# Last eight output blocks with the last pair included, and key products of a recurrence on GpSimd

## The chip, the cores and the metric

The kernel runs on one core of one Trainium2 chip. The metric is device time in microseconds of that core, for one launch that takes all weights and tables from HBM.

## The reference, cut to what matters

The model has two blocks on 256 tokens of width 2048, in float32. The first block (a mixture of gating, short convolution and dilated attention, then a wide MLP) is not touched. The second block is

```python
h = rmsnorm(x, norm1_w); p = h @ w_in
z_rwkv, q, k, v = jnp.split(p, IN_SPLITS, axis=-1)
y_rwkv = rwkv7_bidir(z_rwkv, ...)                  # 16 heads of 64, forward and backward
y_attn = axial_gqa(q, k, v, q_norm_w, k_norm_w)    # 16 query heads, rotary embedding
x = x + jnp.concatenate([y_rwkv, y_attn], axis=-1) @ w_out
h2 = rmsnorm(x, norm2_w)
x = x + peer_ffn(h2, w_pq, sub_keys, u_tab, v_tab)
out = rmsnorm(x, normf_w)
```

Inside the recurrence the keys of a direction are `k_dir = k * (1 + (a - 1) * k_a)` and `ka = kk * a`, with `a` a sigmoid for each direction; the bonus takes the mean of `k_dir` over both directions. The rotary embedding is `x * cos + rotated(x) * sin`.

## The kernel before, in words

The residual x lies transposed: 16 tiles of 128 features by 256 tokens. A projection to 128 features is a "block": `stage` loads 128 x 1024 weights at a time with a DMA from SP (four buffers), ACT rounds them to a high part wH and DVE subtracts it to get the low part wL (L334, L335; three buffers of each), and `product` multiplies: the inputs are stored as pairs of a high and a low part, so that each 128-row step takes one matmul of 512 columns with wH (L344) and one of 256 columns with wL (L346), all into one accumulator of PSUM (two of them, tag acc).

Program order is not the order on the engines: a scheduler lays out each engine's queue ahead of time from priorities (program order at first) and its own costs, and each engine then runs its queue strictly in that order, with semaphores where data are needed.

The second block, in program order: projections of keys and values of the attention (two key blocks with rotary embedding, `rope`), low-rank inputs, then eight pairs of heads p = 0 to 7. For a pair there are three generators that are advanced by the string PLAN: C is the recurrence itself (`rwkv_chain`), B prepares the next pair's matrices (`rwkv_prep`), A makes the projections for the pair after that and its attention heads (`feed`, `gqa`). In `rwkv_prep`, for each direction, the decay is summed by a matmul (L875) and exponentiated on ACT (L882, L884), the keys are formed (L888 on ACT, then products, tile ak), two sets of small matmuls take them (L902 to ms, L909 transposes), and M, ATK and so on are stored for the chain. `tt` is an elementwise operation of two tensors (L251 in the profile); its engine is DVE unless one is named.

For pairs 6 and 7, where nothing is left to project, the places of A are taken by the output projection (`out_blocks`): its first 16 blocks (wo2a) take the eight attention tiles, the next 16 (wo2b) take the first seven pairs; two blocks run at each place, and what is left runs after the chain of pair 7. Then the last pair's result is split into its high and low parts, and 16 one-wide products (wo2c) add it. After each of them `n4.add` scales the finished tile of x (ACT L400, DVE L401) and sums its square over features: ACT squares it (L407) and two matmuls with ones add it up (L411); two buffers of squares alternate by the parity of the tile. Next come the query blocks of the expert layer (wpq, 16 steps each), which take all 16 scaled tiles, and the blocks of the expert table (ut).

Of the kernel before, what the change touches and what calls it, by code (L numbers as in the profile page):

```python
# [28 lines left out]
ADD, SUB, MUL = ALU.add, ALU.subtract, ALU.mult  # L29

P = 128
# [5 lines left out]
NS = 10  # L37
PLAN = "BCCBAABCABCAC"
OUTS = 2
GATED = 2  # L40
PRI = 300
AHEAD = 4
# [30 lines left out]
    ORD1 += [("c", _i, 14 + _i), ("x", _i, 20 + _i), ("b", _i, 8 + _i)]  # L73
KORD1 = list(range(10, 16)) + list(range(0, 10))

ORD2 = [("gk", 0, 37), ("gk", 1, 38), ("gv", 0, 39), ("gv", 1, 40)]
ORD2 += [("lo", _i, 24 + _i) for _i in range(3)] + [("gl", _i, 27 + _i) for _i in range(2)]
for _i in range(8):
# [87 lines left out]
def pack_inputs(inp):  # L166
    A = {k: np.asarray(v) for k, v in inp.items()}
    asc = np.ascontiguousarray
    r = {}

    def cols(v):
        return v.reshape(-1, P).T

    def dup(v):
        return np.concatenate([v.reshape(64, 1), v.reshape(64, 1)], 0)

    def blocks(w, order=None):
        kk, n = w.shape
        b = w.reshape(kk // P, P, n // P, P).transpose(2, 1, 0, 3)
        return b if order is None else b[order]  # L180

    r["xT"] = asc(A["x"][0].T.reshape(16, P, T).transpose(1, 0, 2))
    parts = {
        "attn_norm": cols(A["attn_norm"][0]), "mlp_norm": cols(A["mlp_norm"][0]),
        "norm1": cols(A["norm1_w_2"][0]), "norm2": cols(A["norm2_w_2"][0]),
        "conv_w": cols(A["conv_w"][0]),
        "qn1": dup(A["q_norm"][0]), "kn1": dup(A["k_norm"][0]),
        "qn2": dup(A["q_norm_w_2"][0]), "kn2": dup(A["k_norm_w_2"][0]),
        "mu_prev": cols(A["mu_prev_2"][0]), "mu_next": cols(A["mu_next_2"][0]),
        "a0": cols(A["a0_2"][0]), "k_k": cols(A["k_k_2"][0]), "k_a": cols(A["k_a_2"][0]),  # L190
        "r_k": cols(A["r_k_2"][0]), "lnx_w": cols(A["lnx_w_2"][0]), "lnx_b": cols(A["lnx_b_2"][0]),
    }
    r["vec"] = asc(np.concatenate([parts[n] for n, _ in _VEC], 1))
    r["w1"] = asc(blocks(A["w_in"][0], [o[2] for o in ORD1]))
    wo = A["w_out"][0].reshape(16, P, 2048)[KORD1].reshape(2048, 2048)
    r["wo1"] = asc(blocks(wo))
    r["wm1"] = asc(blocks(A["w_mlp_in"][0]))
    r["wm2"] = asc(A["w_mlp_out"][0].reshape(4, 16, P, 16, P).transpose(0, 3, 2, 1, 4))
    r["w2"] = asc(blocks(A["w_in_2"][0], [o[2] for o in ORD2]))
    wo2 = blocks(A["w_out_2"][0])  # L200
    r["wo2a"], r["wo2b"] = asc(wo2[:, :, 8:]), asc(wo2[:, :, :7])
    r["wo2c"] = asc(wo2[:, :, 7].transpose(1, 0, 2))
    r["wpq"] = asc(blocks(A["w_pq_2"][0]))
    r["ut"] = asc(A["u_tab_2"][0].reshape(P, P, 16, P).transpose(0, 3, 2, 1))
    for n in range(2):
        r[f"vt{n}"] = asc(A["v_tab_2"][0][:, n * 1024:n * 1024 + 1024])
    r["gf"] = asc(np.broadcast_to(A["normf_w_2"], (P, 2048)))
    r["sgw"] = asc(A["sgu_w"][0].transpose(2, 0, 1))
    r["sgb"] = asc(A["sgu_b"][0])
    r["skT"] = asc(A["sub_keys_2"][0].reshape(16, P, P).transpose(2, 0, 1))  # L210


    lora = np.zeros((8, P, 10, P), np.float32)
    w2, a2, g2 = A["w2_2"][0], A["a2_2"][0], A["g2_2"][0]

    def put(slot, r0, src):
        lora[:, r0:r0 + src.shape[0], slot, :] = src.reshape(src.shape[0], 8, P).transpose(1, 0, 2)

    put(0, 0, w2[0])
    put(1, 96, w2[1][:32])  # L220
    put(2, 0, w2[1][32:])
    put(3, 64, a2[0][:64])
    put(4, 0, a2[0][64:])
    put(5, 32, a2[1])
    put(6, 0, np.broadcast_to(A["w0_2"][0][0], (P, 1024)))
    put(7, 0, np.broadcast_to(A["w0_2"][0][1], (P, 1024)))
    put(8, 0, g2[:P])
    put(9, 0, g2[P:])
    r["lora"] = lora
    c = _consts()  # L230
    for n, names in (("cg", C_G), ("c1", C_1), ("cr", C_R), ("ch", C_H), ("cp", C_P)):
        r[n] = _pack(names, c)
    return r
# [6 lines left out]
def mega(tc, a, out):  # L240
# [150 lines left out]
    class Norm:  # L391


        def __init__(self, pool, gname, by_pe=False):
            self.pool, self.g, self.xs, self.acc, self.by_pe = pool, gname, [], None, by_pe

        def scale(self, j):
            x, g = cur["x"], vcol(self.g, j)
# [5 lines left out]
        def square(self, j, sq=None):  # L404
            if sq is None:
                sq = self.pool.tile([P, T], F32, name=nm("sq"), tag="ssq" if (j % 2 if self.by_pe else j == 0) else "nsq", bufs=1)
            S.activation(sq, cur["x"][j], AF.Square)  # L407
            if self.by_pe:
                if self.acc is None:
                    self.acc = ps((P, T))  # L410
                TE.matmul(self.acc, ones, sq, start=j == 0, stop=j == 15)  # L411
            elif self.acc is None:
                self.acc = sq
            else:
                tt(self.acc, self.acc, sq, ADD)
# [284 lines left out]
    def rope(d, o, q):  # L700
        s = ps((P, T))
        TE.matmul(s, cr["rot"], d, start=True, stop=True)
        tt(q, s, cr["sin"], MUL)
        tt(o, d, cr["cos"], MUL)
        tt(o, o, q, ADD)

    def gqa(i):
# [121 lines left out]
    def rwkv_prep(p, r, k, vpad, sws, aas):  # L829
# [41 lines left out]
        for d in range(2):  # L871
            sw, aa = sws[d], aas[d]
            cum = prep((P, 2, P))
            for t_ in range(2):
                TE.matmul(cum[:, t_], sw[:, t_], cr["trif" if d == 0 else "trib"], start=True, stop=True)  # L875
            cv = cum.rearrange("p a (b t) -> p (a b) t", b=2)
            pp = pr.tile([P, 4, 65], F32, name=nm("pp"), tag="pp")
            edge = 0 if d == 0 else 64
            V.memset(pp[:, :, edge:edge + 1], 1.0)
            cur = pp[:, :, 1:65] if d == 0 else pp[:, :, 0:64]  # L880
            prv = pp[:, :, 0:64] if d == 0 else pp[:, :, 1:65]
            S.activation(cur, cv, AF.Exp, scale=-DECAY)  # L882
            pi = c4(scr[("ra", "rb")[d]])
            S.activation(pi, cv, AF.Exp, scale=DECAY)  # L884
            V.tensor_copy(pc[:, d], pp[:, :, 64 - edge])

            kd = (bon, kd2)[d]
            S.activation(kd, aa, AF.Identity, bias=omka[:, p:p + 1], scale=vcol("k_a", p))  # L888
            tt(kd, kd, k, MUL)
            tt(aa, aa, kk, MUL)  # L890
            ak = pr.tile([P, 4, 3, 64], F32, name=nm("ak"), tag="ak")
            tt(ak[:, :, 0], c4(aa), pi, MUL)
            tt(ak[:, :, 1], c4(kd), pi, MUL)
            S.copy(ak[:, :, 2], ak[:, :, 0])
            if d == 1:
                tt(bon, bon, kd, ADD)
            tt(kr_[:, d, :, 0], c4(kk), prv, MUL)
            tt(kr_[:, d, :, 1], c4(r), cur, MUL)
            ms = [prep((P, 4, 2, 64)) for _ in rows]
            for c in range(4):  # L900
                for h, b in enumerate(rows):
                    TE.matmul(ms[h][:, c], ak[b, c, h:h + 2, :], kr_[b, d, c], start=True, stop=True)  # L902
            for h, b in enumerate(rows):
                tt(M[:, d, h], ms[h], ptm[:, d].unsqueeze(1).to_broadcast([P, 4, 2, 64]), MUL)

            tr = [prep((P, 4, P)) for _ in rows]
            for c in range(4):
                for h, b in enumerate(rows):
                    TE.transpose(tr[h][:, c], ak[:, c, h:h + 2, :].rearrange("p k t -> p (k t)"), ident)  # L909
            for h, b in enumerate(rows):  # L910
                S.copy(ATK[:, d, h], tr[h][:, :, b])
            if d == 0:
                yield
# [174 lines left out]

    def out_blocks(x):

        for name, ks in (("wo2a", range(8, 16)), ("wo2b", range(7))):
            for j in range(16):
                if j == 0:
                    reload(ks)
                if name == "wo2a":
                    nc.sync.dma_start(x[j], xd[j])
                acc = block(a[name][j], [y2[k] for k in ks])
                add_to(x[j], acc)
                yield
# [50 lines left out]
        for c in "CBA":  # L1150
            run(gens[c])
    run(outs)
    parts = stage(a["wo2c"], 16)
    last = split(yb[1])
    for j in range(16):
        H, L = (z[:, j % 8:j % 8 + 1] for z in parts[j // 8])
        acc = product([(H, L)], [last])
        add_to(x[j], acc)
        n4.add(j)
    rstd = n4.rstd()  # L1160
    closep(pr, psI, psP)
    psS = openp("psS2", bufs=6, space=PSUM)
# [91 lines left out]
    A = {}  # L1254
# [349 lines left out]
    with tc.If(over > R1):  # L1604
# [3 lines left out]
        for h in range(2):  # L1608
# [1 line left out]
    closep()  # L1610


_NAMES = ["xT", "vec", "w1", "wo1", "wm1", "wm2", "w2", "wo2a", "wo2b", "wo2c", "wpq", "ut", "vt0", "vt1", "gf", "sgw", "sgb", "skT",
          "lora", "cg", "c1", "cr", "ch", "cp"]


# [17 lines left out]
```

## Time and profile before

| | |
|---|---|
| median of 3 runs | 3029.47 us (3025.51 to 3030.99) |
| profiled execution | 3029.49 us |
| its span | 3027.3 us, 51482 instructions |
| busy PE, DVE, ACT, GpSimd | 2986.1, 2176.4, 1725.4, 373.7 us |
| granted clock of TensorE, mean | 0.995 |

The span runs from the first to the last instruction. PE is TensorE's matmuls, PEld its weight loads, DVE is VectorE, ACT ScalarE, POOL GpSimd, SP the engine that issues most transfers. A row such as `sl<-sl,acc` names the tile written and the tiles read. Ends of matmuls are modelled, so what one matmul costs is read from the start of one to the start of the next. The second block's recurrence fills about 1190 to 1690 us, the expert layer what follows.

### The profile page before, as it was taken

To read this page: it belongs to the slowest core of one execution; us is meant where nothing else is said; L and a number is where in the kernel's file an instruction comes from. 1 tells how busy PE (TensorE), PEld (TensorE's weight loads), DVE (VectorE), ACT (ScalarE), POOL (GpSimd) and SP (SyncE) were. 2 spreads that over 40 slices of the span, in tenths; PEclk is the share of its full clock that TensorE was granted. 3 is DMA by queue.
4 is the path that set the end of the run, shared out by engine and by line. 5 is a ranking of instruction groups with operands and counts; after the bars stand their busy time and mean duration, and the time that the engine had idled before them with its cause. 6 is when DMAs were issued, how large, how long until landed. Compare 5 with 4: busy or idle time off the path is not lost. (4 is left out here: it accounts for less than half of the span.)

```text
span 3027.3 us, 51482 instructions
## 1 busy us (share of the span) xinstructions
PE 2986.1 (99%) x19222; PEld 2548.6 (84%) x19222; DVE 2176.4 (72%) x4407; ACT 1725.4 (57%) x3077; POOL 373.7 (12%) x354
## 2 busy tenths in 40 slices
PE   9999999999999999999999999999999999999998
PEld 7888888888888888788787788898888888788886
DVE  7767665655656667778787799989966766666666
ACT  6644554454535546767664544688645454655655
POOL 0000000000000000000000000000053331555553
PEclk9999999999999999999999999999999999999999
DMA  6455555555555665222243455567799997888885
GB/s 222 151 163 191 189 187 190 187 192 188 190 189 187 204 202 170 97 90 97 85 132 114 156 175 181 182 231 235 255 288 280 291 266 233 290 279 289 278 278 193
DMA packets 215508, 605.00 MB, mean 200 GB/s; under 512 B 21904, under 2 KB 79888, under 8 KB 212944
## 3 DMA queue, kind: packets, MB, share of 16 engines
q1 hardware_dynamic: 179248, 475.96, 49.6%
q0 software_dynamic: 36000, 125.65, 11.9%
q8 instruction: 153, 2.51, 0.3%
q14 instruction: 107, 0.88, 0.1%
HBM read 562.01 MB, written 39.52 MB: 199 GB/s over the span
## 5 line engine op out<-in xcount | busy, mean ns | idle before, releaser
L344 PE MATMUL acc<-sl,wH 128*128 128x512 f32 x6192 | 1539.9, 396 | 9.6 <-ACT wH L334 4.3
L344 PEld LDWEIGHTS acc<-sl,wH 128*128 128x128 f32 x6192 | 1132.9, 189 | 236.4 <-ACT wH L334 6.3
L334 ACT CAST wH<-raw 128x1024 fp32r<-128x1024 f32 (+1 forms) x780 | 816.5, 1048 | 733.0 <-PE acc L344 612.1
L335 DVE TENSOR_TENSOR wL<-raw,wH 128x1024 fp32r<-128x1024 f32 (+1 forms) x780 | 931.1, 1220 | 380.1 <-issue 196.0
L346 PEld LDWEIGHTS acc<-sl,wL 128*128 128x128 f32 x6192 | 802.0, 191 | 35.2 <-issue 3.2
L346 PE MATMUL acc<-sl,wL 128*128 128x256 f32 x6192 | 828.5, 284 | 0.0
L251 DVE TENSOR_TENSOR wL<-raw,wH 128x1024 fp32r<-128x1024 f32 x212 | 259.4, 1225 | 141.6 <-ACT wH L1563 139.4
L1563 ACT CAST wH<-raw 128x1024 fp32r<-128x1024 f32 x212 | 222.8, 1052 | 176.3 <-PE acc L1572 86.6
L1561 POOL DMA_INDIRECT raw<-in_vt_dram,A x208 | 238.6, 1147 | 188.5 <-DVE z L251 78.7
L1572 PE MATMUL y<-wH,z 128*128 128x512 f32 x904 | 259.3, 395 | 0.0
L1474 POOL DMA_INDIRECT rows<-A,slots x126 | 133.2, 1057 | 949.8 <-DVE A L1473 749.1
L1572 PEld LDWEIGHTS y<-wH,z 128*128 128x128 f32 x904 | 169.8, 188 | 39.6
L1071 POOL MEMSET vp<- 128x64 f32 x8 | 1.2, 153 | 1483.5 <-ACT rs L382 1100.6
L1572 PE MATMUL y<-wL,z 128*128 128x512 f32 x452 | 141.5, 394 | 0.0
L1572 PEld LDWEIGHTS y<-wL,z 128*128 128x128 f32 x452 | 84.9, 188 | 20.7
L1572 PE MATMUL acc<-wH,z 128*128 128x512 f32 x304 | 94.0, 391 | 0.0
L251 DVE TENSOR_TENSOR sl<-hd,sl 128x256 fp32r<-128x256 f32 x64 | 27.3, 426 | 92.8 <-ACT sl L368 92.8
L352 ACT COPY A<-acc 128x256 f32<-128x256 f32 x126 | 46.8, 371 | 73.6 <-PE acc L346 71.4
L1352 ACT ACTIVATE og<-og,sl 128x128 f16<-128x128 f16 x256 | 87.3, 392 | 1.3 <-DVE og L251 0.8
L251 DVE TENSOR_TENSOR A<-A,gb 128x256 f32<-128x256 f32 x126 | 52.9, 420 | 23.0 <-ACT A L1267 21.5
L1572 PEld LDWEIGHTS acc<-wH,z 128*128 128x128 f32 x304 | 57.1, 188 | 12.7
L251 DVE TENSOR_TENSOR x<-x,acc 128x256 f32<-128x256 f32 x160 | 66.4, 415 | 0.0
(412 smaller groups left out, 2652.5 us busy)
## 6 DMA issues: line engine op xcount, KB each, us to landing
raw<-in_wm_dram SPq DMA_DIRECT2D x256, 512.0 KB, 4.4
raw<-in_ut_dram SPq DMA_DIRECT2D x256, 512.0 KB, 5.2
raw<-in_w_dram SPq DMA_DIRECT2D x170, 512.0 KB, 4.2
raw<-in_wo_dram SPq DMA_DIRECT2D x32, 512.0 KB, 4.3
raw<-in_wpq_dram SPq DMA_DIRECT2D x32, 512.0 KB, 4.4
gates<-gst SPq DMA_DIRECT2D x16, 1024.0 KB, 7.1
gb<-gates SPq DMA_DIRECT2D x16, 1024.0 KB, 9.1
raw<-in_wo2a_dram SPq DMA_DIRECT2D x16, 512.0 KB, 3.4
```

The costliest lines, as they stand in the source:

```text
L251: eng.tensor_tensor(o, x, y, op=op)
L334: S.copy(H, raw)
L335: cur["split"] = V.tensor_tensor(L, raw, H, op=SUB)
L344: TE.matmul(acc, halves[k // 8][0][:, k % 8], xs[k].rearrange("p a t -> p (a t)"), start=k == 0, stop=False)
L346: TE.matmul(acc[:, :T], halves[k // 8][1][:, k % 8], xs[k][:, 0], start=False, stop=k == n - 1)
L352: S.copy(d, b)
L1071: G.memset(d[:, 0:64], 0.0)
L1352: S.activation(gL[:, t], o1[:, t], AF.Copy, scale=glo[:, t0 + t:t0 + t + 1])
L1474: i = G.indirect_dma_start(out=rows, out_offset=bass.IndirectOffsetOnAxis(ap=slots[:, e:e + 1], axis=0), in_=z[:, 0:2 * P + 1], in_offset= ...
L1561: G.indirect_dma_start(out=raw, out_offset=None, in_=a[f"vt{c2}"], in_offset=off)
L1563: ins = S.copy(H, raw)
L1572: TE.matmul(y[h][2 * c2 + c], lhs, w[:, c * 512:c * 512 + 512], start=h not in seen and k == 0, stop=n == last[h] and k == 2)
```

## The change

Three edits.

First, the output projection. wo2b is now made for its first eight blocks only (EARLY = 8). The last eight have matrices of eight steps (wo2d) that include the last pair; each of them stands in front of one of the one-wide products that remain for the first eight blocks, so that tiles of x are finished in the order 8, 0, 9, 1, ... 15, 7 (KORD2). The rows of wpq and ut are stored in that order, since the scaled tiles are now in it. The one-wide products use the accumulators of tag prep. The sum of squares counts its own steps to know the first and the last.

Second, in `rwkv_prep` the products that form the keys (`kd`, `aa`, two parts of `ak`, and the sum into `bon` in the second direction) run on GpSimd instead of DVE.

Third, in `rope` the product with the cosine runs on GpSimd.

```diff
+EARLY = 8
+KORD2 = [_j + _n for _j in range(EARLY) for _n in (EARLY, 0)]
...
-    r["wo2a"], r["wo2b"] = asc(wo2[:, :, 8:]), asc(wo2[:, :, :7])
-    r["wo2c"] = asc(wo2[:, :, 7].transpose(1, 0, 2))
-    r["wpq"] = asc(blocks(A["w_pq_2"][0]))
-    r["ut"] = asc(A["u_tab_2"][0].reshape(P, P, 16, P).transpose(0, 3, 2, 1))
+    r["wo2a"], r["wo2b"], r["wo2d"] = asc(wo2[:, :, 8:]), asc(wo2[:EARLY, :, :7]), asc(wo2[EARLY:, :, :8])
+    r["wo2c"] = asc(wo2[:EARLY, :, 7].transpose(1, 0, 2))
+
+    r["wpq"] = asc(blocks(A["w_pq_2"][0])[:, :, KORD2])
+    r["ut"] = asc(A["u_tab_2"][0].reshape(P, P, 16, P).transpose(0, 3, 2, 1)[:, :, KORD2])
...
-                TE.matmul(self.acc, ones, sq, start=j == 0, stop=j == 15)
+                TE.matmul(self.acc, ones, sq, start=self.n == 0, stop=self.n == 15)
+                self.n += 1
...
-        tt(o, d, cr["cos"], MUL)
+        tt(o, d, cr["cos"], MUL, G)
...
-            tt(kd, kd, k, MUL)
-            tt(aa, aa, kk, MUL)
+            tt(kd, kd, k, MUL, G)
+            tt(aa, aa, kk, MUL, G)
             ak = pr.tile([P, 4, 3, 64], F32, name=nm("ak"), tag="ak")
-            tt(ak[:, :, 0], c4(aa), pi, MUL)
-            tt(ak[:, :, 1], c4(kd), pi, MUL)
+            tt(ak[:, :, 0], c4(aa), pi, MUL, G)
+            tt(ak[:, :, 1], c4(kd), pi, MUL, G)
             S.copy(ak[:, :, 2], ak[:, :, 0])
             if d == 1:
-                tt(bon, bon, kd, ADD)
+                tt(bon, bon, kd, ADD, G)
...
-            for j in range(16):
+            for j in range(16 if name == "wo2a" else EARLY):
...
-    parts = stage(a["wo2c"], 16)
-    last = split(yb[1])
-    for j in range(16):
-        H, L = (z[:, j % 8:j % 8 + 1] for z in parts[j // 8])
-        acc = product([(H, L)], [last])
-        add_to(x[j], acc)
-        n4.add(j)
+    (H, L), = stage(a["wo2c"], EARLY)
+    y2[7] = split(yb[1])
+    for j in range(EARLY):
+
+        for n in KORD2[2 * j:2 * j + 2]:
+            if n == j:
+                acc = product([(H[:, j:j + 1], L[:, j:j + 1])], [y2[7]], prep())
+            else:
+                acc = block(a["wo2d"][j], y2[:8])
+            add_to(x[n], acc)
+            n4.add(n)
```

## Rows read from the trace of the kernel before

**Rows 1.** The page, part 1: busy us (share of the span) xinstructions.

```profile
PE 2986.1 (99%) x19222; PEld 2548.6 (84%) x19222; DVE 2176.4 (72%) x4407; ACT 1725.4 (57%) x3077; POOL 373.7 (12%) x354
```

**Rows 2.** Table by stage: PE, PEld, DVE, ACT, POOL busy (x); PEclk; DMA share; GB/s.

```profile
1190.00:1640.00 450.00, 445.38 (x4780) 359.26 (x4779) 349.33 (x871) 296.60 (x738) 1.39 (x12) 1.00 0.32 104
1672.04:1691.67 19.63, 19.63 (x112) 17.27 (x113) 14.69 (x27) 7.46 (x8) 0.00 (x0) 1.00 0.67 214
1691.67:1720.30 28.63, 24.61 (x98) 17.52 (x97) 23.20 (x54) 18.35 (x40) 0.00 (x0) 0.88 0.23 74
```

**Rows 3.** Waits of PE in 1190 to 1640: us in total, times, longest.

```profile
PE ps_inv L943 <- DVE bd L251: 0.9, 2, 0.4
```

**Rows 4.** Time line of PE, 1643 to 1726: start, us, what, [idle before].

```profile
1643.55 1.20 PE L344 MATMUL acc<-sl,wH 128*128 128x512 f32 x4
...
1672.04 1.84 PE L344 MATMUL acc<-sl,wH 128*128 128x512 f32 x7 [0.36 <-DVE sl L251]
...
1698.39 0.59 PE L411 MATMUL ps<-sq,cg 128*128 128x256 f32 x2
1698.63 0.59 PE L344 MATMUL acc<-sl,wH 128*128 128x512 f32 x1
...
1720.30 3.82 PE L344 MATMUL acc<-sl,wH 128*128 128x512 f32 x16
...
1725.87 0.61 PE L1244 MATMUL ps<-skT,sl 128*128 128x128 f32 x4
```

**Rows 5.** Groups in 1691.67 to 1720.3: busy us, mean ns, idle before.

```profile
L251 DVE TENSOR_TENSOR sl<-sl,acc 128x256 f32<-128x256 f32 x34 | 13.7, 418 | 1.9 <-PE acc L346 1.6
L401 DVE SCALAR_TENSOR_TENSOR sl<-sl,vec,sl 128x256 fp32r<-128x256 f32 x16 | 7.7, 479 | 0.6 <-ACT sl L400 0.6
L335 DVE TENSOR_TENSOR wL<-raw,wH 128x1024 fp32r<-128x1024 f32 x4 | 4.9, 1224 | 3.3 <-ACT rs L378 2.7 <-ACT wH L334 0.6
...
L400 ACT ACTIVATE sl<-sl,vec 128x256 fp32r<-128x256 f32 x16 | 8.1, 507 | 9.4 <-DVE sl L251 9.3
...
L334 ACT CAST wH<-raw 128x1024 fp32r<-128x1024 f32 x5 | 5.2, 1049 | 2.2 <-PE acc L344 2.1
```

**Rows 6.** Time line of one set of keys, all engines, 1412 to 1417.

```profile
1412.49 0.60 ACT L888 ACTIVATE sl<-aa,omka,vec 128x256 f32<-128x256 f32 x1
...
1413.58 0.43 DVE L251 TENSOR_TENSOR sl<-sl,rk 128x256 f32<-128x256 f32 x1
...
1414.59 0.43 DVE L251 TENSOR_TENSOR ak<-aa,sl 128x256 f32<-128x256 f32 x1
...
1415.71 1.83 PE L902 MATMUL ps<-kr,ak 64*128 64x128 f32 x16
1415.93 0.41 ACT L894 COPY ak<-ak 128x256 f32<-128x256 f32 x1
```

**Rows 7.** Time line, the split of the last pair, 1669 to 1675.

```profile
1670.26 0.41 ACT L368 CAST sl<-sl 128x256 fp32r<-128x256 f32 x1 [0.88 <-DVE sl L251]
...
1673.47 0.42 DVE L251 TENSOR_TENSOR sl<-sl,sl 128x256 fp32r<-128x256 f32 x1
```

**Rows 8.** The page, part 6: transfers of a wide block, KB, us to landing.

```profile
raw<-in_wo2a_dram SPq DMA_DIRECT2D x16, 512.0 KB, 3.4
```

**Rows 9.** The page, part 5: GpSimd's groups.

```profile
L1561 POOL DMA_INDIRECT raw<-in_vt_dram,A x208 | 238.6, 1147 | 188.5 <-DVE z L251 78.7
...
L1071 POOL MEMSET vp<- 128x64 f32 x8 | 1.2, 153 | 1483.5 <-ACT rs L382 1100.6
```

**Rows 10.** Time line, rotary embedding of the second key block, 1121 to 1124.

```profile
1121.66 0.42 DVE L251 TENSOR_TENSOR sl<-sl,cr 128x256 f32<-128x256 f32 x1
1121.99 1.22 DVE L335 TENSOR_TENSOR wL<-raw,wH 128x1024 fp32r<-128x1024 f32 x1
...
1123.69 0.67 PE L767 MATMUL ps<-sl,cr 128*128 128x256 f32 x2 [2.31 <-DVE sl L251]
```

**Rows 11.** Groups of DVE in 1190 to 1640.

```profile
L335 DVE TENSOR_TENSOR wL<-raw,wH 128x1024 fp32r<-128x1024 f32 x69 | 83.9, 1221 | 9.1 <-PE acc L346 5.9 <-ACT sl L378 2.2 <-ACT ATK L911 0.8
```

More of the change, by code (lines that the diff above doesn't have):

```diff
@@ L394, in __init__ @@
         def __init__(self, pool, gname, by_pe=False):
-            self.pool, self.g, self.xs, self.acc, self.by_pe = pool, gname, [], None, by_pe
+            self.pool, self.g, self.xs, self.acc, self.by_pe, self.n = pool, gname, [], None, by_pe, 0
         def scale(self, j):
@@ L1610, in mega @@
     closep()
-_NAMES = ["xT", "vec", "w1", "wo1", "wm1", "wm2", "w2", "wo2a", "wo2b", "wo2c", "wpq", "ut", "vt0", "vt1", "gf", "sgw", "sgb", "skT",
+_NAMES = ["xT", "vec", "w1", "wo1", "wm1", "wm2", "w2", "wo2a", "wo2b", "wo2c", "wo2d", "wpq", "ut", "vt0", "vt1", "gf", "sgw", "sgb", "skT",
           "lora", "cg", "c1", "cr", "ch", "cp"]
```

## The prediction

> **What bounds the kernel now.** I read the page first: TensorE (PE) is busy for 2986.1 us of the span, 99% [rows 1]; no other engine comes near. So the sum is only about stretches in which PE does not issue its matmuls back to back, and those I looked for in the table by stage [rows 2]. Three of its rows matter. In 1190 to 1640, the middle of the recurrence, PE is busy 445 of 450 us and DVE 349: the waits that the profile puts down to other engines there are eight rows of at most 0.9 us, about 4 us together (the largest is shown, [rows 3]). In 1672.04 to 1691.67 PE runs eight seven-wide output blocks without a gap. In 1691.67 to 1720.30, the last pair's 16 one-wide products and the first query block, PE is busy only 24.6 of 28.6 us, and its clock falls to a mean 0.88, so about 6.9 us of it run at 1.2 instead of 2.4 GHz. That stage is the loose one.
>
> The profiled execution took 3029.49 us (span 3027.3 and 2.2 around it), the median of the runs is 3029.47, so no correction lies between them.
>
> **Part 1, the last eight output blocks.** The number of matmuls stays: eight blocks of 7 and eight of 1 become eight of 8. What changes is what stands beside the one-wide products.
>
> Prices on PE. A seven-wide block: 19.63/8 = 2.45 us [rows 2], 0.35 a step; a 16-wide query block 1725.87 - 1720.30 = 5.57 us, also 0.35 a step [rows 4]. So a one-wide product is 0.35, an eight-wide block 2.79. The two matmuls that sum the squares of one block: 1698.63 - 1698.39 = 0.24 us [rows 4].
>
> Stage now: 16 x 0.35 + 16 x 0.24 + 5.57 = 15.0 us of PE work in 28.63 us. So 13.6 us are lost to waits and to the low clock: in each step PE waits for the sums of the accumulators, 34 additions on DVE of 0.42 us in a chain with ACT's scaling [rows 5], and there is nothing else for PE to do.
>
> Stage after, per pair (one block of 8, one product of 1, two sums of squares): PE 2.79 + 0.35 + 0.49 = 3.63 us. DVE for the same pair: four additions, two scalings, one weight split, 4 x 0.418 + 2 x 0.479 + 1.224 = 3.85 us by durations [rows 5]; but instructions that follow each other overlap by some 0.09 us (0.34 apart at 0.43 us each, [rows 6]), which makes 3.2. ACT needs 2 x 0.51 for scaling, two squares of about the same and one cast of 1.05 [rows 5, 6], about 3.1. So PE is the bound by a small margin, and DVE is near. From the end of the eighth wo2b block, 1672.04 [rows 4], the kernel now takes 19.63 + 28.63 = 48.3 us to the end of the first query block; with PE back to back it takes 8 x 3.63 + 5.57 = 34.6. That is -13.7 us. Against it stand:
> - The last pair is now needed earlier. The first eight-wide block reaches its eighth step 7 x 0.24 = 1.7 us after its start (3.82/16 a step, [rows 4]), at 1673.7. The split of the last pair is cast on ACT at 1670.26 and ends on DVE at 1673.47 + 0.42 = 1673.9 [rows 7]; it could end at 1671.1. Between 0 and 1.5 us, I take 0.5. What covers the chain of the last pair is then eight blocks instead of sixteen, the same eight that cover it now (1643.55 to 1672.04, [rows 4]).
> - DVE so near to PE: 0 to (3.85 - 3.63) x 8 = 1.8 us, I take 1.0, as additions queue behind splits.
> - The end: the last block's sums, scaling and remainder (about 2.2 us with the last product's additions in between) stand behind 14 steps of the first query block (14 x 0.24 = 3.3 us), unless a weight split of 1.22 us goes ahead of them. 0 to 2 us, I take 1.0.
>
> Loads: SP issues eight transfers of 512 KB in place of eight of 448 KB, and one of 512 KB less; such a transfer lands in 3.4 us [rows 8], within one pair's 3.63 us, and four buffers hold them. The weights of the one-wide products hold one of three split buffers, now two; the remaining two are enough at one eight-wide block each. The order of the rows of wpq and ut changes on the host: no time. Part 1: -13.7 + 2.5 = -11.2 us (bounds -13.7 to -8.4).
>
> **Part 2, nine products and sums per pair on GpSimd (72 in all).** DVE loses 72 x 0.34 = 24 us of issue time. PE is the bound there, and only the 4 us of waits can come back: the gain is at most 4. The price on GpSimd is in no row: below stands its 64-column memset, 0.153 us; above, its indirect transfer's 1.147 us [rows 9]. Four times the memset, for four times the columns, is 0.61 us; I take that, as the nearer row. The Trainium skill gives a price in "GPSIMD Engine Reference", section 3.1: 4497 ns for a sum of 2048 columns, an estimate of 0.56 us for our 256; no row here shows it, and the sum would be the same.
>
> Four of them stand in a row ahead of PE's 16 small matmuls of keys (L902). Now [rows 6]: the input from ACT is there at 1412.49 + 0.60 = 1413.09, DVE starts at 1413.58 (behind a split), ends at 1414.59 + 0.43 = 1415.02; but the copy on ACT that the matmuls also need starts only at 1415.93, and PE begins at 1415.71. GpSimd has no queue: 1413.09 + 4 x 0.61 = 1415.53, still ahead of that copy. So I take 0. Upper bound: four at 1.147 end at 1417.7, 1.7 us after the copy's start now, 16 sets of keys: +28 us. Lower bound -4. Queued behind a late key on PE are the whole filler blocks; on GpSimd behind it only the next keys, and the zeroing of two borders per pair of 0.15 us each.
>
> **Part 3, one product of the rotary embedding (10 of them).** It leaves DVE's chain and runs beside the rotation matmul. It shows only where PE has no filler, at the second key block [rows 10]: DVE multiplies with the sine and then, at 1121.66, with the cosine, then a split of 1.22 us goes ahead of the sum, and PE waits until 1123.69. With the second product elsewhere the sum can start at 1121.66, and PE at 1122.1: -1.6 us. If the split still goes first it is -0.3. If the product on GpSimd takes 1.15 us the sum still starts at about 1121.7. I take -1.0 (bounds 0 to -1.6).
>
> Sum: -11.2 + 0 - 1.0 = -12.2 us: 3029.5 - 12.2 = 3017.3, forecast **3017 us**.
>
> **The rivals.**
> - Keys late (slower). Place: PE ahead of each of the 16 sets of key matmuls; price: what GpSimd is late. It decides from 12.2/16 = 0.76 us a set: more than that, and the gain of parts 1 and 3 is gone. If a product takes 0.95 us, four end at 1416.9, 1.0 after the copy now, and that copy, the third thing behind, adds its 0.41: 1.4 x 16 = 22 us, 3040. For it: ahead of these matmuls there is no slack now [rows 6]. Against: there are filler blocks to put in front, and it needs products half as long again as my estimate.
> - Products and DVE shut each other out. If GpSimd's reading and DVE's two-input work cannot overlap, each product may wait for a split of 1.22 us (69 of them in this stretch, [rows 11]). DVE's splits fill 84 of 450 us, its other two-input products about as much; so about a third of the products waits, half a split each: four take 4 x 0.61 + 1.3 x 0.61 = 3.2 us, ending at 1416.3, and 0.4 plus the copy's 0.41 late: 0.8 x 16 = 13 us, 3030. "SBUF — State Buffer", section "Who interferes with whom", of the Trainium skill says so: a VectorE instruction with two SBUF inputs and a GpSimd instruction that reads SBUF exclude each other for the whole instruction. No run yet shows the two together.
> - The pairs run at DVE's pace. If each pair takes 4.5 us, as sums of squares share one buffer between the two blocks of a pair and additions wait behind splits, 8 x 0.87 = 7 us come back: 3023 or so. For it: DVE and ACT are at 3.2 and 3.1 of 3.63 us.
> - More comes back: all bounds of the gain, -13.7 - 1.6 - 4 = -19: 3010.
> - The change does not do what it says: the order on each engine is worked out anew, and the wide blocks may be drawn to other places. It has no price of its own; it is in the range.
>
> **How the numbers follow.** Forecast 0.60 (3012 to 3022); more comes back 0.10 (3008 to 3012); DVE's pace 0.14 (3021 to 3026, 0.05 of it still beyond the limit); shut out 0.05 (3030); keys late 0.11 (3036 and more). A difference under 0.2%, 6 us, cannot be told from none here. Faster (below 3023.4): 0.60 + 0.10 + 0.05 = 0.75; within: 0.09 + 0.05 = 0.14; slower: 0.11. The range leaves out the keys that come very late and a little of the best case: 3009 to 3031.
>
> **What would show it.** Part 1: no row of PE waiting for DVE or ACT longer than 0.5 us between the wide blocks, pairs 3.6 to 3.8 us apart, granted clock 1.00 in the stage, 35 to 37 us from the eighth wo2b block to the end of the first query block. Part 2: GpSimd's products near 0.6 us, PE's waits ahead of L902 no longer than now, DVE some 24 us less busy. Part 3: PE's wait ahead of L767 at 1 us or less. The prediction is wrong if PE waits for GpSimd at L902 by a microsecond each time, or if pairs take over 4.2 us.

## The result, and the profile after

| | median, us | runs | ratio to before, 95% interval |
|---|---|---|---|
| before | 3029.47 | 3025.51 to 3030.99 | |
| predicted | 3017 | range 3009 to 3031 | |
| after | 3060.55 | 3059.14 to 3065.10 | 1.0112 [1.0100, 1.0124] |

The changed kernel is 31 us slower: the wrong sign, outside the range. The profiled execution after has a span of 3060.2 us against 3027.3. In the code after, line 251 (the helper that records DVE's and GpSimd's products and sums) is L254, the products on PE are L347 and L349, the key matmuls L906, the rotary sum's reader L771.

The place of the loss is found by starts that both traces have:

| mark on PE | before | after | difference |
|---|---|---|---|
| sum of the second key block read (L767, L771) | 1123.69 | 1121.39 | -2.3 |
| last group of pair 7's recurrence starts (L1048, L1052) | 1661.54 | 1702.97 | +41.4 |
| first score matmul (L1244, L1253) | 1725.87 | 1757.03 | +31.2 |
| end of the span | 3027.3 | 3060.2 | +32.9 |

So part 3 brought something, the recurrence lost 44 us, the last output blocks gave 10 back, and the rest of the kernel is as before to within 2 us. The page's part 1 of the kernel after, to be read beside [rows 1] (busy us, share of the span, instructions):

```profile
PE 2997.3 (98%) x19222; PEld 2559.2 (84%) x19222; DVE 2159.5 (71%) x4308; ACT 1722.7 (56%) x3076; POOL 454.2 (15%) x436
```

The whole page hides it: PE still reads 98%. Its middle, in the table by stage of the kernel after (columns as in [rows 2]), does not:

```profile
1190.00:1640.00 450.00, 420.02 (x4276) 337.15 (x4274) 310.33 (x730) 274.92 (x690) 69.04 (x89) 0.96 0.29 94
1712.99:1752.14 39.15, 39.15 (x213) 33.36 (x212) 31.96 (x66) 24.93 (x48) 0.00 (x0) 1.00 0.46 148
```

In the recurrence PE is busy 420.0 us where it was 445.4 [rows 2], and its granted clock falls to 0.96: seven stretches at 1.2 instead of 2.4 GHz, 37.5 us together, none there before. The second row is the stage of part 1, from the end of the eighth wo2b block to the end of the first query block: 39.2 us where it was 48.3, without a gap and at the full clock.

What PE waits for in 1190 to 1690 of the kernel after, the largest three (us in total, times, longest; [rows 3] was the largest before):

```profile
PE ps L906 <- POOL ak L254: 20.7, 9, 3.4
PE ps L906 <- DVE kr L254: 3.9, 4, 1.4
PE ps L906 <- ACT rk L700: 2.1, 2, 1.1
```

All three are the keys. From PE's time line, the time from the start of the matmul ahead to the first key matmul, summed over the 16 sets, is 32.7 us; before it was 3.7.

GpSimd's groups in 1050 to 1760 of the kernel after (count | busy us, mean ns of one | idle before, releasers):

```profile
L254 POOL TENSOR_TENSOR aa<-aa,sl 128x256 f32<-128x256 f32 x16 | 17.0, 1068 | 118.8 <-DVE sl L254 118.8
L254 POOL TENSOR_TENSOR ak<-sl,sl 128x256 f32<-128x256 f32 x16 | 15.6, 976 | 0.0
L254 POOL TENSOR_TENSOR sl<-sl,rk 128x256 f32<-128x256 f32 x16 | 13.8, 863 | 185.6 <-ACT sl L892 178.3 <-DVE zp L698 3.4 <-ACT wH L337 2.4
L254 POOL TENSOR_TENSOR ak<-aa,sl 128x256 f32<-128x256 f32 x16 | 12.5, 782 | 60.4 <-ACT sl L888 53.8 <-PE acc L349 6.6
L254 POOL TENSOR_TENSOR sl<-sl,sl 128x256 f32<-128x256 f32 x8 | 5.9, 732 | 0.2
```

A product takes 0.73 to 1.07 us in the mean, not 0.61. And DVE's groups of the same form changed although nothing in their code did. First the kernel after, then the one before, both in 1190 to 1690:

```profile
L254 DVE TENSOR_TENSOR zp<-zp,rstd 128x256 f32<-128x256 f32 x21 | 10.9, 521 | 0.0
L254 DVE TENSOR_TENSOR kr<-rr,pp 128x256 f32<-128x256 f32 x16 | 10.8, 674 | 0.0
L254 DVE TENSOR_TENSOR zp<-acc,zp 128x256 f32<-128x256 f32 x21 | 8.7, 416 | 0.4 <-ACT zp L355 0.3
```

```profile
L251 DVE TENSOR_TENSOR kr<-rr,pp 128x256 f32<-128x256 f32 x16 | 6.7, 422 | 0.0
```

The product kr, with both inputs in SBUF, went from 422 to 674 ns. zp<-acc,zp, whose first input acc lies in PSUM, stays at 416. I sorted DVE's instructions of this stretch by whether a GpSimd product ran during any of their time. Products and sums of two 128x256 tiles in SBUF take 420 ns alone (88) and 694 beside one (29, longest 978); the weight split 1219 alone (52) and 1455 beside (16, longest 1757); a 128x256 product or sum with a PSUM input 418 alone (161) and 414 beside (16). GpSimd's product is at 0.72 us alone and reached 1.7. So the two engines hold each other up when both read SBUF; DVE's work with a PSUM input kept its time. It is not only two-input work: DVE's small copies from SBUF to SBUF (128x4, L889) take 0.17 us alone and up to 0.71 beside a product.

One set of keys in the time line of all engines after (start, us, what [idle before]); this is where it was read before: [rows 6]:

```profile
1429.75 1.03 POOL L254 TENSOR_TENSOR sl<-sl,rk 128x256 f32<-128x256 f32 x1 [11.30 <-ACT sl L892]
...
1430.74 0.90 POOL L254 TENSOR_TENSOR aa<-aa,sl 128x256 f32<-128x256 f32 x1
...
1430.99 1.74 DVE L338 TENSOR_TENSOR wL<-raw,wH 128x1024 fp32r<-128x1024 f32 x1
...
1431.61 1.70 POOL L254 TENSOR_TENSOR ak<-sl,sl 128x256 f32<-128x256 f32 x1
...
1433.27 0.72 POOL L254 TENSOR_TENSOR ak<-aa,sl 128x256 f32<-128x256 f32 x1
...
1434.04 1.91 PE L906 MATMUL ps<-kr,ak 64*128 64x128 f32 x16 [3.04 <-POOL ak L254]
```

The third product and the split run over each other; one takes 1.70 us and the other 1.74. The row that I had priced at 2.44 us lasts from 1429.75 to 1433.99, 4.24 us, and PE stands for 3.04 us. One of the seven low stretches of the clock starts at 1435.17, just after it.

### The profile page after: what moved, and what is told of

The parts are those of the page before. It is cut to its first block, busy times and chain, and to the rows that moved or that the text cites. A ratio compares the mean times of both kernels' runs of the same rounds, so it can differ in the third digit from the quotient of the medians.

```text
span 3060.2 us, 51485 instructions
## 1 busy us (share of the span) xinstructions
PE 2997.3 (98%) x19222; PEld 2559.2 (84%) x19222; DVE 2159.5 (71%) x4308; ACT 1722.7 (56%) x3076; POOL 454.2 (15%) x436
## 4 chain that ended last, share of the span: by engine, by line
PE 82%; issue 7%; DVE 6%; ACT 2%; POOL 2%; DMA 2%; DVEq 0%; POOLq 0%; SPq 0%; ACTq 0%
PE acc L347 39%; PE acc L349 20%; PE y L1581 10%; PE acc L1581 3%; DVE wL L338 2%; PE ps L906 1%; PE ps L913 1%; POOL rows L1483 1%; POOL ak L254 1%; DVE sl L254 1%; POOL aa L254 0%; PE ps_inv L947 0%; PE ps L1363 0%; PE ps L1362 0%; PE ps L742 0%
## 5 line engine op out<-in xcount | busy, mean ns | idle before, releaser
L347 PE MATMUL acc<-sl,wH 128*128 128x512 f32 x6184 | 1538.1, 396 | 7.5 <-ACT wH L337 3.2
L347 PEld LDWEIGHTS acc<-sl,wH 128*128 128x128 f32 x6184 | 1130.0, 189 | 231.8 <-issue 6.4
L349 PEld LDWEIGHTS acc<-sl,wL 128*128 128x128 f32 x6184 | 801.5, 192 | 35.4 <-issue 4.2
L349 PE MATMUL acc<-sl,wL 128*128 128x256 f32 x6184 | 828.1, 285 | 0.1
L254 DVE TENSOR_TENSOR wL<-raw,wH 128x1024 fp32r<-128x1024 f32 x212 | 259.1, 1224 | 142.1 <-ACT wH L1572 91.2
L1483 POOL DMA_INDIRECT rows<-A,slots x126 | 140.1, 1112 | 830.1 <-ACT wH L337 601.8
L1581 PEld LDWEIGHTS y<-wL,z 128*128 128x128 f32 x452 | 84.8, 188 | 21.2 <-DVE wL L254 0.6
L254 DVE TENSOR_TENSOR sl<-hd,sl 128x256 fp32r<-128x256 f32 x64 | 27.3, 427 | 92.8 <-ACT sl L371 92.8
L254 DVE TENSOR_TENSOR A<-A,gb 128x256 f32<-128x256 f32 x126 | 52.8, 419 | 23.0 <-ACT A L1276 21.6
L254 DVE TENSOR_TENSOR x<-x,acc 128x256 f32<-128x256 f32 x160 | 66.3, 414 | 0.0
```

The source lines that it names most:

```text
L254: eng.tensor_tensor(o, x, y, op=op)
L347: TE.matmul(acc, halves[k // 8][0][:, k % 8], xs[k].rearrange("p a t -> p (a t)"), start=k == 0, stop=False)
L349: TE.matmul(acc[:, :T], halves[k // 8][1][:, k % 8], xs[k][:, 0], start=False, stop=k == n - 1)
L1483: i = G.indirect_dma_start(out=rows, out_offset=bass.IndirectOffsetOnAxis(ap=slots[:, e:e + 1], axis=0), in_=z[:, 0:2 * P + 1], in_offset= ...
L1581: TE.matmul(y[h][2 * c2 + c], lhs, w[:, c * 512:c * 512 + 512], start=h not in seen and k == 0, stop=n == last[h] and k == 2)
```

## The experiments

Differences are between the medians of the kernel and of the one before, measured side by side on the same chip. The kernel before took 3023.9 to 3027.3 us there, and the times in the expectations start from its 3029.5, so it is the differences that compare.

**Each edit by itself.** Theory: edit 2, the keys, makes the whole loss. Rival: the edits collide only together, or the new order of the queues costs as a whole.

> The kernel before with the first edit alone (last eight output blocks take the last pair along). Theory 'keys late' (the whole loss lies in the keys on GpSimd, PE standing in front of their matmuls): 3018 to 3021 us, that is 9 to 11 us faster, as the stretch behind the recurrence shows in the changed kernel. Theory 'order' (the new plan of the queues is worse as a whole, whoever makes the keys): no gain, 3027 us or more.

> The kernel before with the second edit alone (keys of the recurrence on GpSimd). 'Keys late': 3070 to 3077 us, 41 to 47 us slower, with PE waiting some 25 us or more in front of L902. 'Order': under 20 us slower, the loss being shared with the other edits.

> The kernel before with the third edit alone (cosine product of the rotary embedding on GpSimd). 'Keys late': 3026 to 3028 us, the 2 to 3 us that PE gains at the second key block. 'Order': anything from 3024 to 3040.

> First and third edit together, keys left on DVE. 'Keys late': 3015 to 3019 us, faster than both kernels. 'Order': 3025 us or more.

The edits are those of the diff of the change: e1 has the blocks alone, e2 the five lines on the keys, e3 the line of the rotary product, e4 both e1 and e3, without the keys.

| | median | difference, us | ratio, 95% interval |
|---|---|---|---|
| e1, blocks | 3016.23 | -8.6 | 0.9971 [0.9960, 0.9982] |
| e2, keys | 3069.44 | +44.7 | 1.0146 [1.0130, 1.0161] |
| e3, rotary product | 3021.63 | -3.2 | 0.9989 [0.9980, 0.9998] |
| e4, blocks and rotary product | 3014.47 | -10.3 | 0.9965 [0.9953, 0.9977] |

The three edits sum to +32.9 and the whole change measured +31.1: they hardly touch each other. Edit 2 makes all of the loss. e3's interval barely leaves 1. e4 is faster than either kernel of this case. What stays open here: edit 2 also gives PE's queue another order, and e2 does not separate the two.

**Why the keys cost 45 us.** Theory A: GpSimd's row is late, and PE, whose order is fixed, stands in front of it. Theory B: GpSimd's reading delays DVE's own work, so it costs even when nobody waits for GpSimd.

> The kernel before, keys on DVE as before, and beside them 64 products of the same inputs on GpSimd whose results (written into the dead tile sw) nobody reads: the same work on GpSimd, nobody waiting for it. 'Keys late': within 5 us of the kernel before, though GpSimd's products again take 0.7 to 1.7 us. 'Exclusion' (the loss comes from DVE's two-input work being shut out by GpSimd's reading): 15 us or more slower.

```
  tt(aa, aa, kk, MUL)
+ tt(nobody, kd, k, MUL, G)
+ tt(nobody, aa, kk, MUL, G)
  ...
  tt(ak[:, :, 1], c4(kd), pi, MUL)
+ tt(c4(nobody), c4(aa), pi, MUL, G)
+ tt(c4(nobody), c4(kd), pi, MUL, G)
```

3054.25 against 3023.85: +30.4 us, 1.0105 [1.0088, 1.0121]. PE's and ACT's queues are, instruction for instruction, those of the kernel before, and no instruction reads the 64 results. PE's waits in 1190 to 1680 of e5, the largest two, and then its table by stage:

```profile
PE ps L914 <- DVE M L251: 10.1, 12, 2.7
PE ps L907 <- DVE kr L251: 9.0, 6, 1.8
```

```profile
1190.00:1640.00 450.00, 420.90 (x4399) 338.02 (x4398) 352.12 (x826) 283.10 (x697) 60.04 (x76) 0.99 0.30 99
```

PE loses 24.5 us of busy time (445.4 to 420.9), nearly as much as in the kernel after, and now it waits for DVE: for the key matmuls' own operand kr and for the matrices M of the recurrence. So an idle product is not free. But it is not true that nobody waits for GpSimd. DVE's waits in 1190 to 1690 of e5 have a row that the kernel before has not:

```profile
DVE sl L251 <- POOL sw L251: 9.2, 6, 3.0
```

In six sets DVE stands in front of its sum into bon until the set's last idle product is done. PE's stands directly behind these waits, each counted up to the length of DVE's wait, are 7.5 of the 10.1 us of the row on M; another 1.8 us stand behind a wait of ACT's for GpSimd: some 9 of PE's 24.5 us. Directly ahead of the rest there is no such wait; DVE's own work got longer (sorted as above, 418 to 685 ns and 1218 to 1483). So e5 shows both theories at work: the mutual slowing, and engines that stand until GpSimd's row is done.

> Keys on GpSimd as in the second edit alone, but with the generator stopping between a direction's keys and their matmuls, and one more B in the plan, so that projection blocks stand on PE between the two. 'Keys late': at least 30 of the 45 us come back, 3040 us or less, PE's waits in front of L902 under 6 us. 'Exclusion': still 3060 or more.

```
- PLAN = "BCCBAABCABCAC"
+ PLAN = "BCCBAABCABCABC"
  ...
+ yield
  ms = [prep((P, 4, 2, 64)) for _ in rows]
```

on top of e2: 3054.45, +30.6 us, 1.0097 [1.0080, 1.0113]. With projection blocks between the keys and their matmuls, PE's largest waits in the stretch are

```profile
PE ps L903 <- POOL ak L251: 7.6, 4, 2.6
PE ps_inv L964 <- DVE Tp L251: 3.5, 5, 2.5
```

So PE's wait for GpSimd falls from 21.2 us in e2 to 7.6, some 14 of 45 us come back, and two thirds of the loss stay. The time lies between the two expectations and meets neither. What stays is not slowed DVE work alone, for DVE itself still waits 8.7 us for GpSimd's sum into bon (four sets).

> Keys on GpSimd as in the second edit alone, and ten idle matmuls of 384 half-precision columns (1.6 us) in front of the key matmuls of each set, into the accumulator that these then overwrite: PE's wait is filled with work. If a good part of the loss is the clock that falls after each long wait, the granted clock stays at 1.00 there and the kernel is 5 to 15 us faster than with the keys alone, 3054 to 3064. If the wait alone costs, the time is the same or longer, 3069 to 3085 (32 sets of 1.6 us are 26 us where there is no wait to fill).

```
+ for _ in range(10):
+     TE.matmul(ms[0].rearrange("p c k t -> p (c k t)")[:, :384], ch["idh"],
+               ch["lvl"][:, :384], start=True, stop=True)
```

ahead of the key matmuls of e2: 3088.67, +64.8 us, 1.0212 [1.0195, 1.0230]. It tells nothing on the clock: the added work is 16 sets of 1.6 us, 26 us (the expectation wrote of 32 sets), the wait for GpSimd stayed at 19.7 us, so the added matmuls did not fill it, and the granted clock of the stretch was 0.97. In the sets with the longest waits they ran some 6 us earlier, 32 to 36 matmuls ahead of the keys.

> Only the chain of kd on GpSimd (two of the four products of a set, and the sum into bon); aa and its product stay on DVE beside it. 'Keys late': the row of two is 0.7 to 0.95 us a product, so a set is late by 0.5 to 1.2 us in place of 2 to 3 and the clock mostly holds: 3030 to 3045 us. 'Exclusion': half the loss, 3045 to 3050.

Only `tt(kd, kd, k, MUL, G)`, `tt(ak[:, :, 1], c4(kd), pi, MUL, G)` and `tt(bon, bon, kd, ADD, G)` are on GpSimd, 40 instructions instead of 72: 3045.01, +21.2 us, 1.0074 [1.0057, 1.0090], about half of e2. This lies where the two expectations meet, so it does not tell them apart. The keys now wait for DVE:

```profile
PE ps L902 <- DVE ak L251: 8.4, 6, 1.9
```

**Is it the reading, or GpSimd being at work?** Theory B says that the exclusion needs GpSimd to read SBUF. Rival: any GpSimd instruction at that place, or the plan of e6, costs.

> The kernel before with idle work on GpSimd again, but such as reads nothing: 128 fillings of the dead tile sw with zero (eight a set, 128 x 256 each) in place of the 64 idle products. 'Exclusion' (what cost 30 us with the idle products is GpSimd's reading, which shuts out DVE's work on two SBUF tiles): within 4 us of the kernel before, DVE's two-input work at its old 0.42 and 1.22 us. If any work on GpSimd costs, through its semaphores or through a new order of the queues: 15 us or more slower.

```
+ for _ in range(4): G.memset(nobody, 0.0)
```

in both places of e5's products: 3026.5 against 3024.36, 1.0004 [0.9995, 1.0014]. 128 fillings, and no difference; the queues of PE, ACT and DVE are those of the kernel before. Beside a filling DVE's 128x256 work on two SBUF tiles takes 417 ns (55) and alone 418 (141), the split 1215 (10) and 1218 (59). The small copies do get longer beside a filling too (0.27 us in the mean, 14), 1.6 us in all. DVE has no wait for GpSimd here, so e9 lacks both things that e5 has. GpSimd's and DVE's group in e9:

```profile
L898 POOL MEMSET sw<- 128x256 f32 x64 | 20.6, 322 | 3.7
```

```profile
L251 DVE TENSOR_TENSOR kr<-rr,pp 128x256 f32<-128x256 f32 x16 | 6.7, 417 | 0.0
```

> Lateness without reading: the four products of each set are left out and eight fillings with zero on GpSimd stand in their place (over kd, aa, the exponential and ak, so that they follow ACT and PE's key matmuls follow them); the keys are zero. DVE is relieved of 64 products as with the keys on GpSimd. 'Keys late' alone: PE again waits 10 us or more in front of L902, 3033 to 3050 us. 'Exclusion' alone: within 5 us of the kernel before or faster, PE's waits there under 4 us.

```
- tt(kd, kd, k, MUL)
- tt(aa, aa, kk, MUL)
+ for z in (kd, kd, aa, aa, scr[("ra", "rb")[d]], scr[("ra", "rb")[d]]):
+     G.memset(z, 0.0)
  ...
- tt(ak[:, :, 0], c4(aa), pi, MUL)
- tt(ak[:, :, 1], c4(kd), pi, MUL)
+ G.memset(ak[:, :, 0], 0.0)
+ G.memset(ak[:, :, 1], 0.0)
```

3024.88, 1.0004 [0.9994, 1.0013], and no wait of PE in front of the key matmuls. But the row was not late: the fillings need no input of DVE's and ran ahead, and the copy that closes a set ended 1.3 us or more before the key matmuls, in seven sets over 30. So e10 did not test lateness.

> The plan of the run with projection blocks between keys and matmuls, with the keys on DVE: what that plan costs by itself. If nothing, 3022 to 3028 us, then the 31 us that were left there are the keys on GpSimd (exclusion and what lateness remained). If 3035 or more, the plan has a cost of its own and the keys on GpSimd cost 20 us or less in it.

e6 with the products back on DVE: 3023.62, 1.0000 [0.9991, 1.0010]. The plan and the yield cost nothing by themselves; what stays in e6 comes with the keys on GpSimd.

> As the run with late writes (keys left out and zero), but with sixteen fillings a set, some 4 us in a row at 0.25 us each: as long as the four products of a set take on GpSimd, and nothing is read. If a long row on GpSimd costs by its length, PE waits 10 us or more in front of L902 and the kernel is 10 to 20 us slower, 3034 to 3045. If the cost of the keys on GpSimd comes from reading alone, within 5 us of the kernel before.

e10 with `[kd]*4 + [aa]*4 + [scr[...]]*4` to fill and each `ak` half twice: 3036.07 against 3027.3, 1.0025 [1.0014, 1.0035]. Sixteen fillings a set make a row about as long as that of the products. GpSimd's first group, and PE's largest wait in 1190 to 1680:

```profile
L890 POOL MEMSET sl<- 128x256 f32 x128 | 39.9, 311 | 383.3 <-ACT sl L884 200.9 <-ACT sl L888 179.5
```

```profile
PE ps L909 <- DVE M L251: 1.0, 4, 0.4
```

PE does not wait for the row, because here too it ran ahead. The copy that closes a row, and the key matmuls after it:

```profile
1370.17 0.40 ACT L894 COPY ak<-ak 128x256 f32<-128x256 f32 x1
...
1409.12 0.81 PE L902 MATMUL ps<-kr,ak 64*128 64x128 f32 x8
```

In 14 of the 16 sets the copy ended over 2 us before the key matmuls. So neither e10 nor e12 says what a late row costs. Two of e12's ten executions took 3027 us, the others 3032 to 3039. The profiled execution of e12 is 7.0 us longer than that of the kernel before: the first score matmul is 2.7 late (1728.57 against 1725.87); some 4 lie in the expert tables long after, where this kernel works on other data, and those I did not follow up.

## Why the prediction was wrong

**Part 2 is the step that failed** ("So I take 0", bounds -4 to +28): e2 measured +44.7. Its steps: a product's price, the room that a set has, and the work and waits of DVE.

- The price and the room. 0.61 us came from four times a 64-column memset [rows 9]. A product is at 0.72 us alone and 0.73 to 1.07 in the mean of its groups. The Trainium skill's figure in "GPSIMD Engine Reference", section 3.1, from which I had estimated 0.56 us, is low as well for this size. With 0.72, four end at 1413.09 + 2.88 = 1415.97 on the scale of [rows 6], level with the copy. But [rows 6] is one set, and one with much room. In six sets of its kind the time from the end of that input from ACT (L888) to PE's key matmuls was 1.9 to 2.6 us before, 2.6 in [rows 6]. In the kernel after PE was at the keys 1.1 to 1.4 us after it in all six, and stood there for 17.4 us. An estimate from these rows: at 0.72 us each, 0.68 apart, four products alone would have kept it there for about 9 us; the other 8 are the rows that took 3.8 to 4.3 us in place of 2.8. Why PE came to the keys earlier, with its queue in another order, no run tests.
- The exclusion. The Trainium skill states in "SBUF — State Buffer", section "Who interferes with whom", that a VectorE instruction with two SBUF inputs and a GpSimd instruction that reads SBUF shut each other out. The traces agree: 420 to 694 ns with two SBUF inputs, 418 and 414 with a PSUM input, and no effect on two-input work from fillings (e9). I had it as a rival, with 13 us and a chance of 0.05. I had counted only what the products wait for DVE's splits, a third of them half a split; I had not counted what DVE's own work loses, beside a product against alone: about 15 us of its time in the kernel after and 23 in e5 (where the products come on top of DVE's own).
- The path behind DVE. I had said "DVE loses 24 us of issue time" and read DVE's 349 of 450 us [rows 2] as slack. But PE takes its instructions in a fixed order, and in this stretch it had only 4 us of waits [rows 3]: a kr or an M that is late by a microsecond is late on PE by that. e5 shows it with the queues of PE and ACT unchanged. DVE also gained a wait of its own, in front of L921, which needs the sum into bon that went to GpSimd; in the kernel after, 1190 to 1690:

```profile
DVE sl L921 <- POOL sl L254: 14.7, 7, 2.7
```

The rival "Keys late" had the place and the sign (GpSimd at L906, 20.7 us in the kernel after), at half the size; by the estimate above the price of a product alone is about half of PE's stand in those six sets.

**What makes up the 45 us.** An accounting of the stretch 1190 to 1640, not an experiment: PE's idle time above that of before (4.6 us), and half of the time that the granted clock was at 1.2 GHz, which is the most that it can cost (between 1190 and 1705). Measured is the profiled execution, from which the other columns are, less the median before:

| | idle more | low clock, us | half of it | sum | measured, profiled execution |
|---|---|---|---|---|---|
| e2, keys | 25.4 | 37.5 | 18.8 | 44.2 | 43.8 |
| after | 25.4 | 37.5 | 18.8 | 44.2 | 41.4 (mark of pair 7) |
| e5, idle products | 24.5 | 6.8 | 3.4 | 27.9 | 27.5 |
| e6, gap | 20.2 | 20.5 | 10.2 | 30.4 | 32.9 |
| e8, half | 12.3 | 6.8 | 3.4 | 15.7 | 18.1 |

The sums are within 3 us, so no other large term is needed. By it, some 25 us of e2 are PE standing and up to 19 the clock; in the kernel after six of its seven low stretches begin in a stand of 2.5 us or more or just after one. In e5 the standing is as long, but in shorter pieces, and the clock fell only once. The clock's own share was not isolated; e7 was meant to and failed. Nor was the standing divided by experiment into price, mutual slowing and DVE's waits for GpSimd; only the estimate above does it, for six sets. Nor do e5's 30 us add to e6's 14 as parts of one sum: in e5 DVE still does its own products, in e2 it does not.

**Part 1 was right in mechanism, 2 to 3 us too good** (-11.2 forecast; -8.6 in e1; -9.1 in the stage, 48.3 to 39.2). Between the wide blocks PE waits once, 0.6 us ahead of the first, and the clock is at 1.00, as forecast; the stage took 39.2 where I had said 35 to 37. PE shows no gap in it, so the terms for DVE's and the last pair's lateness did not come as waits. The term that was too small is PE's price of the sums of squares, the 0.24 us of [rows 4]:

```profile
1746.39 0.59 PE L414 MATMUL ps<-sq,cg 128*128 128x256 f32 x2
1746.63 0.59 PE L347 MATMUL acc<-sl,wH 128*128 128x512 f32 x1
1747.06 0.60 PE L414 MATMUL ps<-sq,cg 128*128 128x256 f32 x2
```

The first matmul of a product behind the sums takes 0.42 us to the next start (0.31 for a narrow one), against 0.23 (0.12) in a row of its kind. That happens 14 times in the stage, 2.7 us; the sums themselves take 4.8 us where 16 x 0.24 are 3.8; and three steps of the second query block, 0.7 us, stand inside the stretch. Together 4.4 of the 4.6 us between 34.6 and 39.2. Why a matmul takes longer there no run shows.

**Part 3 was right in mechanism and too small** (-1.0 forecast; -3.2 in e3). The wait ahead of the second key block is gone. The time line after, answering [rows 10]:

```profile
1119.05 1.58 POOL L254 TENSOR_TENSOR sl<-sl,cr 128x256 f32<-128x256 f32 x1 [5.41 <-PE acc L349]
...
1120.66 0.42 DVE L254 TENSOR_TENSOR sl<-sl,sl 128x256 f32<-128x256 f32 x1
1121.39 0.59 PE L771 MATMUL ps<-sl,cr 128*128 128x256 f32 x2
```

The sum starts as soon as GpSimd is done, ahead of the next split, which was my best case of -1.6; it starts there although the product took 1.58 us beside a split. The low stretch of the clock that followed the wait, 3.4 us from 1124.7 on, is gone in the kernel after, in e3 and in e4; I had not counted it, and it is worth at most 1.7 us.

## What to carry to other kernels

Before work goes from VectorE to GpSimd, look in the trace at what VectorE does at those times: if both read SBUF, an instruction of VectorE that meets a product gets longer (here by some 0.25 us in the mean with two SBUF inputs), so does the product, and a busy share of 78% is no slack when the engine behind it takes its work in a fixed order. Then ask for each moved instruction who waits for it, and for each delayed one too, and read the room in front of the reader in every place and not in one. An idle copy of the moved work, with the original left in place, shows in one run that it interferes; look in its waits whether another engine stands for it all the same.

## What the runs showed of the hardware that was not expected

- 64 products of 128x256 on GpSimd that nobody reads cost 30.4 us of 3024 (e5), in part through DVE's waits for them (9.2 us); 128 fillings of the same size there cost nothing that can be told from zero (e9).
- The weight split on DVE, 128x1024 with two SBUF inputs, went from 1219 to 1455 ns beside a product, up to 1757; a product on GpSimd went from 0.72 to as much as 1.7 us there and 2.6 in e5. DVE's products and sums with a PSUM input did not change. DVE's 128x4 copies in SBUF went from 0.17 to as much as 0.71 us beside a product and 0.38 beside a filling.
- PE's granted clock fell to 1.2 GHz for 3.4 or 6.8 us at a time seven times in the recurrence of the kernel after, one of them 1.1 us after a stand of 3.04 us. In e5, with nearly as much standing in pieces of at most 2.7 us, it fell there once.
- A matmul of 512 columns directly behind the two matmuls that sum squares took 0.42 us to the next start, against 0.23 in a row (ten times in the last output blocks of the kernel after).
